# Heads and tails of the stages of a decoder-layer kernel: metered weight loads, a reordered projection loop, up-projections in a drain and a longer prologue

## The chip, the cores and the metric

One Trainium2 chip, 8 cores, one launch. Each core takes one sequence of a batch of 8, so all cores run the same program on different data and exchange nothing. The metric is the device time of the slowest core in microseconds (us), as the median of several executions. An eight-core program has a slower state in some of its executions: the cores of one die, or of both, show a lower granted TensorE clock. Those runs are left out of every comparison below; all profiles that are quoted fell in the fast state.

## The reference, cut to what matters

A decoder layer on `x` (8, 4096, 1024) in float32, with three sub-layers, each behind an RMS norm:

```python
# 1. two token mixers on one normalised input
qa, ka, va, ra, za, qb, kb, vb = split(rms_norm(x, norm_mix) @ w_in)
log_a = log_sigmoid(za @ w_gla_gate + b_gla_gate) / 16          # low-rank decay, rank 16
o_a = gla_chunked(qa * dk**-0.5, ka, va, log_a)                 # gated linear attention, 4 heads
o_a = rms_norm(o_a, gla_out_norm) * silu(ra)
qd = rope_partial(rms_norm(qb, dil_q_norm)); kd = rope_partial(rms_norm(kb, dil_k_norm))
o_b = dilated_attention(qd, kd, vb)                             # 3 groups of 8 heads of 64
h = x + (g_a * (o_a @ w_br_gla) + g_b * (o_b @ w_br_dil)) @ w_mix_out
# 2. attention from 4 heads of 256 into 256 memory tokens
k, v = split(rms_norm(mem, norm_mem) @ w_xkv)
h = h + softmax(rms_norm(norm(h) @ w_xq) @ rms_norm(k).T) @ v @ w_xo
# 3. gated MLP, 2816 wide, with a causal convolution of width 3 ahead of gelu
h = h + (gelu(conv(norm(h) @ w_a)) * (norm(h) @ w_u)) @ w_ffn_down
```

## The kernel before

A small helper `fw` records every operation with its buffers and sets the semaphores; each engine then runs its own instructions in the order in which the program wrote them. That order is therefore all the scheduling there is. Loads of activations are issued by SyncE, loads of weights by GpSimd (`q="pool"`). The 4096 tokens are 32 tiles, called chunks in the linear attention, of 128; four make a slab of 512. The stages follow one another: prologue, linear attention (32 chunks), dilated attention, merge, memory attention, FFN. The parts that the change touches:

```python
# prologue: x, all early weights (6 MB of them), and only then the small gains
for i in range(3):
    nload(i)
...
for h in range(4):
    fw.dma(wqk[h]..., q="pool")            # 4 x 512 KB, q and k of the linear attention
for j in range(4):
    fw.dma(wvr[j]..., q="pool")            # 4 x 1 MB, values and swish gate
... gains ...
for i in range(8):                         # normalise two slabs
    nstat(i); nscale(i); ntrans(i); nload(i + 3)
    if i == 3: P_za(0)                     # low-rank decay, first half
    if i == 4: P_z(0)                      # and its 8 activations
for h in range(4):
    P_e(0, h)                              # scan of the decay (DVE), two exps (ACT)
    P_qk(0, h)                             # q and k projection, multiplied by the exps

# linear attention
for c in range(NT):
    hs_ = ((), (0,), (1, 2), (3,))[c4] if nx else ()
    R_o(c)                                 # output and state of chunk c
    for h in hs_:
        P_e(s_ + 1, h)
    if nx and c4 == 0:
        P_za(s_ + 1)
    R_r(c + 1)                             # swish gate of the next chunk
    ...
    R_on(c)                                # norm of the output times gate
    for h in hs_:
        P_qk(s_ + 1, h)
    R_v(c + 1, 0); R_a(c + 1); R_v(c + 1, 1)   # values and scores of the next chunk
    ...

# first projection of the dilated stage is prepared at the last chunk
CC["gqk"] = rc_.sb("gqk", (128, 2, 8, 64), F32)      # gain of 64 values, for 8 heads and 128 partitions
for a_ in range(2):
    fw.dma(CC["gqk"][:, a_, :, :], bass.AP(..., [[0, 128], [0, 8], [1, 64]]), join=True)

# merge stage: keys and values of the memory, in slots between other work
def kv_alloc(isv):
    fw.dma(KV["w"]..., q="pool")           # 2 MB in one transfer
def kv_norm(m):
    fw.dma(mt[:, :], mem[rows(m), :])      # loaded and used in the same slot
    fw.act(junk, mt, AF.Square, accum=...)
```

After memory attention the FFN's buffers are allocated and its weights loaded; no up-projection starts before the last output projection.

Of the kernel before, what the change touches and what calls it, by code (L numbers as in the profile page):

```python
# [436 lines left out]
def build():  # L437
# [31 lines left out]
    pers = Reg(Arena(nc, LO, HI - LO), 0, 4608)  # L469
# [4 lines left out]
    gall = pers.sb("gall", (128, 140), F32)  # L474
    AB = pers.p
# [131 lines left out]
    CC = {}  # L607

    def load_wd(k, g):
        wd = ar.at("wd%d" % k, (128, 8, 3, 512), BF16, (64 + 24 * (k % 2)) * K_)  # L610
        for kc in range(0, 8, 2):
            fw.dma(wd[:, kc:kc + 2, :, :].rearrange("p c j n -> p (c j n)"),
                   V(WD["w_dil"], WD["w_dil"].t[g][:, kc * 1536:(kc + 2) * 1536]), q="pool", join=True)
        CC["wd%d" % g] = wd

    GORD = (1, 2, 0)

    def c_early():
        load_wd(0, GORD[0])
        CC["tab"] = ar.at("tabc", (128, 6, 512), F32, 120 * K_)  # L620
        fw.dma(CC["tab"][:, :, :], rope_d.full_v())

# [176 lines left out]
    for i in range(3):  # L799
        nload(i)  # L800
    for h in range(4):
        fw.memset("pool", U[h][:, :], 0.0)
    fw.dma(wz[:, :, :].rearrange("p c n -> p (c n)"), WD["w_gz"].full_v(), q="pool")
    fw.dma(wgg[:, :], SM["w_gla_gate"].full_v(), q="pool")
    fw.dma(posf[:, :], pos.full_v(), q="pool")
    for h in range(4):
        fw.dma(wqk[h][:, :, :, :].rearrange("p c w n -> p (c w n)"), V(WD["w_gqk"], WD["w_gqk"].t[h]), q="pool")
    for j in range(4):
        fw.dma(wvr[j][:, :, :].rearrange("p c n -> p (c n)"), V(WD["w_gvr"], WD["w_gvr"].t[j]), q="pool")
    gr0 = 0  # L810
    for nm_, n_ in gnames:
        src = SM[nm_].full_v()
        if nm_ == "w_ffn_conv":
            src = src.rearrange("t n -> (t n)")
        gdst = grow[gr0:gr0 + n_, :] if gr0 < 52 else grow2[gr0 - 52:gr0 - 52 + n_, :]
        fw.dma(gdst, src.rearrange("(c p) -> c p", p=128), join=True)
        gr0 += n_
    fw.dma(gon[:, :], dram_bc(SM["gla_out_norm"], 256))
    gps = PB.next()
# [4 lines left out]
    fw.ts("dve", gon[:, :], gon[:, :], 0.5, ALU.mult)  # L824
    for i in range(8):
# [4 lines left out]
        if i == 3:  # L830
            P_za(0)
        if i == 4:
            P_z(0)
    Gr = Reg(ar, g_off, g_off + 8 * K_).ring("G", 2, (128, 1024), F32)
    for h in range(4):
        P_e(0, h)
        P_qk(0, h)
# [9 lines left out]
    def c_alloc():  # L847
# [6 lines left out]
        CC["gqk"] = rc_.sb("gqk", (128, 2, 8, 64), F32)  # L854
# [8 lines left out]
        for a_ in range(2):  # L863
            nm = "dil_q_norm" if a_ == 0 else "dil_k_norm"
            a = SM[nm].t
            fw.dma(CC["gqk"][:, a_, :, :], V(SM[nm], bass.AP(a.tensor, a.offset, [[0, 128], [0, 8], [1, 64]])), join=True)
# [27 lines left out]
    def proj(it, j):  # L894
# [17 lines left out]
        fw.tt("dve", c["qg"][:, j, :, :], p_[:, :].rearrange("p (a d) -> p a d", a=8), CC["gqk"][:, j, :, :], ALU.mult,  # L912
# [73 lines left out]
    for c in range(NT):  # L986
        s_, c4 = c // 4, c % 4
        nx = s_ + 1 < NS
        i = c + 8
        hs_ = ((), (0,), (1, 2), (3,))[c4] if nx else ()  # L990
        R_o(c)
        for h in hs_:
            P_e(s_ + 1, h)
        if nx and c4 == 0:
            P_za(s_ + 1)
        if c + 1 < NT:
            R_r(c + 1)
# [11 lines left out]
        for h in hs_:  # L1009
            P_qk(s_ + 1, h)  # L1010
        if c + 1 < NT:
            R_v(c + 1, 0)
            R_a(c + 1)
            R_v(c + 1, 1)
        if i + 1 < NT:
# [10 lines left out]
        if c == 27:  # L1026
            c_early()

# [87 lines left out]
    def c_step(step):  # L1116
        i, j, k = step, step - 2, step - 3
        ok = lambda q: 0 <= q < N_
        d = step - N_
        if i == 32 + 4:  # L1120
# [59 lines left out]
    fw.dma(wmo[:, :, :].rearrange("p c n -> p (c n)"), WD["w_mo"].full_v(), q="pool")  # L1180
# [31 lines left out]
    def kv_alloc(isv):  # L1212
        KV["w"] = ar.at("wkv%d" % isv, (128, 8, 1024), BF16, 0)
        fw.dma(KV["w"][:, :, :].rearrange("p c n -> p (c n)"), V(WD["w_xkv"], WD["w_xkv"].t[isv]), q="pool")

    def kv_alloc2():
        KV["mt"] = ar.at("mt", (128, 1024), F32, 16 * K_)
        KV["mn"] = ar.at("mnT", (128, 8, 256), BF16, 20 * K_)
        KV["gk"] = ar.at("gkx", (128, 256), F32, 85 * K_)
        fw.dma(KV["gk"][:, :], dram_bc(SM["x_k_norm"], 256))  # L1220

    def kv_norm(m):
        mt = KV["mt"]
        fw.dma(mt[:, :], mem[rows(m), :])
# [3 lines left out]
        xs = ogc["xs"].next()  # L1228
        fw.ts("dve", xs[:, :], mt[:, :], ss[:, 2:3], ALU.mult)
        KV["xs%d" % m] = xs  # L1230

    def kv_trans(m):
        pt = trans8(P.next(), KV["xs%d" % m])
# [19 lines left out]
    def kv_k(m):  # L1253
# [7 lines left out]
        kn = ogc["xs"].next()  # L1261
        for h in range(4):
            fw.stt("dve", kn[:, h * 256:(h + 1) * 256], srcs[h], ss[1][:, h:h + 1], KV["gk"][:, :], ALU.mult, ALU.mult)
        KV["kn"] = kn

    def kv_kt(m):
        pt = trans8(P.next(), KV["kn"])
        fw.copy("act", KV["kmT"][:, :, m * 128:(m + 1) * 128], pt)

    def kv_wxq():  # L1270
        KV["wxq"] = ar.at("wxq", (128, 8, 1024), BF16, 0)
        for kc in range(0, 8, 4):
            fw.dma(KV["wxq"][:, kc:kc + 4, :].rearrange("p c n -> p (c n)"),
                   V(WD["w_xq"], WD["w_xq"].t[:, kc * 1024:(kc + 4) * 1024]), q="pool", join=True)

    def kv_wxo():
        KV["wxo"] = ar.at("wxo", (128, 8, 1024), BF16, 32 * K_)
        for kc in range(0, 8, 4):
            fw.dma(KV["wxo"][:, kc:kc + 4, :].rearrange("p c n -> p (c n)"),
                   V(WD["w_xo"], WD["w_xo"].t[:, kc * 1024:(kc + 4) * 1024]), q="pool", join=True)  # L1280

    kv_plan = {(4, 1): [lambda: kv_alloc(0), kv_alloc2, lambda: kv_norm(0)],
               (4, 2): [lambda: kv_trans(0), lambda: kv_norm(1)], (4, 4): [lambda: kv_trans(1), kv_alloc3],
               (5, 0): [lambda: kv_k(0)], (5, 2): [lambda: kv_kt(0), lambda: kv_k(1)],
               (5, 4): [lambda: kv_kt(1), lambda: kv_alloc(1)], (6, 2): [lambda: kv_v(0)],
               (6, 4): [lambda: kv_v(1)], (6, 6): [kv_wxq]}
    for s_ in range(NS):
        for m in range(8):
# [29 lines left out]
            for f_ in kv_plan.get((s_, m), ()):  # L1318
                f_()

# [6 lines left out]
    gq = rx.sb("gqx", (128, 256), F32)  # L1327
# [6 lines left out]
    fw.dma(gq[:, :], dram_bc(SM["x_q_norm"], 256))  # L1334
# [13 lines left out]
    XL = {}  # L1348

# [37 lines left out]
    def q_norm(i):  # L1387
        c = TC[i]
        qn = qn2r.next()
        for h in range(4):  # L1390
            fw.stt("dve", qn[:, h * 256:(h + 1) * 256], c["qs"][h], c["ss"][:, 8 + h:9 + h], gq[:, :],
# [84 lines left out]

    x2load(0)
    x2load(1)
    fw.dma(gfb[:, :], dram_bc(SM["norm_ffn"], 1024))
    for k in range(NT + 11):  # L1480
        if k < 5:
# [5 lines left out]
            if k == 3:  # L1487
                kv_wxo()
# [33 lines left out]
        if NT + 1 <= k < NT + 5:  # L1522
            up_load(13 + k - NT - 1)


    for fc in range(17, NFC):
        up_load(fc)
    x3t = F_["x3"]
    wdn = ar.at("wdn", (128, NFC, 1024), BF16, 64 * K_)
    wdsub = [wdn.sub("wdn%d" % j) for j in range(6)]  # L1530
    for j in range(6):
        c0, c1 = j * 4, min(NFC, j * 4 + 4)
        fw.dma(V(wdsub[j], wdn.t[:, c0:c1, :]).rearrange("p c n -> p (c n)"),
               V(WD["w_dn"], WD["w_dn"].t[:, c0 * 1024:c1 * 1024]), q="pool")
    yt_ = ar.at("yT", (128, NFC, 512), BF16, 108 * K_)
    ysub = [yt_.sub("yT%d" % fc) for fc in range(NFC)]
    rf = Reg(ar, 52 * K_, 64 * K_)
    c1r = rf.ring("cv1_", 2, (128, 512), F32)
    c2r = rf.ring("cv2_", 2, (128, 512), F32)
    glr = rf.ring("gl", 2, (128, 512), F32)  # L1540
    abr = Reg(ar, 44 * K_, 49 * K_).ring("abt", 2, (128, 514), F32)
    rf = Reg(ar, 130 * K_, 150 * K_)
    h2r = rf.ring("h2f", 4, (128, 1024), F32)
    hist = rf.sb("hist", (128, NFC, 2), F32)
    hsub = [hist.sub("hist%d" % fc) for fc in range(NFC)]
    for fc in range(NFC):
        fw.memset("pool", V(hsub[fc], hist.t[:, fc, :]), 0.0)
    PB = Rot(BK)
    wcb = V(gall, gall.t[:, 52:140])

# [105 lines left out]
```

## Time and profile before

| | before |
|---|---|
| median of 3 runs | 3181.96 us (3180.67 to 3182.05) |
| spans of the 8 cores, profiled execution | 3162.8 to 3178.1 us, mean 3170.7 |
| granted TensorE clock | 0.976 to 0.982 |
| PE busy on the slowest core | 2904.7 us, 91% |

Where PE stands still is in the prediction below, line by line. Two more views help. The first is PE's timeline (start and duration in us, the operation, how many; in brackets the idle time before it and what ended it), in one chunk of the linear attention of the kernel before:

```profile
221.13 3.40 PE L245 MATMUL psum<-xnT,wqk_52 128*128 128x512 bf16 x15
...
229.27 0.27 PE L245 MATMUL psum<-qe_3_76,ke_3_80 128*128 128x128 bf16 x1 [2.84 <-DVE ke_3_80 L278]
```

The last head's projection is followed by 1.9 us of value matmuls and then by the scores that need this head's keys. DVE has not yet evacuated them, and PE waits 2.84 us. The second view is the list of transfers of the whole execution (count, size of each, median us from issue to landing):

```profile
xt_61<-x SPq DMA_DIRECT2D x11, 512.0 KB, 3.8
...
gqk<-dil_q_norm SPq DMA_DIRECT2D x1, 256.0 KB, 17.1
```

Half the bytes took more than four times as long: the gain table is written as 1,024 pieces of 256 bytes. Part of its 17.1 us it shared with 3 MB of weights; the run gqk_wide_late below has the table without them.

To know where the time goes I cut every core's execution at PE's own landmarks. "Chunk 0" is the first output matmul of chunk 0; the other marks are first or last matmuls of a kind. The figures for all runs are in the ledger under "The result". For the kernel before: 90.4 us to chunk 0, 73.0 for chunks 0 to 3, 388.9 for chunks 4 to 27, 83.9 from chunk 28 to the first transposes of the dilated attention, 646.8 for its projections and scores, 580.7 for the merge stage, 81.4 from the first query projection of memory attention to its first output projection, 377.2 from there to the first down-projection of the FFN.

### The profile page before, as it was taken

What the parts mean: (1) busy time and instruction counts of PE and PEld (TensorE: products, weight loads), DVE (VectorE), ACT (ScalarE), POOL (GpSimd) and SP (SyncE); (2) the same over time, 40 slices, a digit from 0 to 9 for tenths busy, and PEclk for the clock granted to TensorE, in tenths of its full rate; (3) what the DMA queues carried; (4) which work ended last, traced back from release to release, by engine and by line L of the source; (5) the groups of instructions that cost most, each with busy time, mean ns of one, the idle gap of its engine ahead of it and who ended that gap; (6) DMA issues with size and microseconds to landing.
All of it is one profiled execution on the core that took longest, in us unless ns stands there. A gap on an engine that the chain in (4) does not pass through costs nothing.

```text
span 3178.1 us, 54582 instructions; the slowest of 8 cores (3162.8 to 3178.1 us)
## 1 busy us (share of the span) xinstructions
PE 2904.7 (91%) x17139; PEld 1465.6 (46%) x17454; DVE 1845.5 (58%) x2994; ACT 1290.9 (41%) x2521; POOL 946.6 (30%) x1434
## 2 busy tenths in 40 slices
PE   3888898599999999899899887999899999999998
PEld 1444444255666555444444443444444444444443
DVE  3666666377676778444344344666656545645744
ACT  2556555266656666522232235665212212211211
POOL 1333333266666677433233210000101100100100
PEclk9999999799999999999999999999999999999999
DMA  7111111511131322544545439446810110110110
GB/s 160 37 52 63 51 34 27 108 37 42 38 82 38 81 77 79 119 147 140 152 138 150 126 131 202 155 152 193 208 67 21 47 67 27 41 67 34 47 54 27
DMA packets 94418, 279.44 MB, mean 88 GB/s; under 512 B 12570, under 2 KB 13750, under 8 KB 89782
## 3 DMA queue, kind: packets, MB, share of 16 engines
q1 hardware_dynamic: 84742, 224.96, 20.3%
q0 software_dynamic: 9392, 50.96, 9.5%
q8 instruction: 145, 2.38, 0.3%
q14 instruction: 139, 1.14, 0.1%
HBM read 224.16 MB, written 102.63 MB: 103 GB/s over the span
## 4 chain that ended last, share of the span: by engine, by line
PE 71%; DVE 10%; issue 6%; ACT 6%; DMA 6%; SPq 0%; POOL 0%; DVEq 0%; ACTq 0%; POOLq 0%
PE psum L245 68%; PE psum L249 3%; ACT jh L271 1%; DMA gqk<-dil_k_norm 1%; DMA xt_61<-x 1%; DVE on_109 L304 1%; ACT junkX L271 1%; DMA oat<-oaT_d 1%; DMA x2i_214<-xn_d 1%; DVE cm_68 L308 1%; DMA mt<-mem 1%; DMA gon<-gla_out_norm 1%; ACT L271 0%; DVE x3s_240 L314 0%; DVE qn_2_222 L304 0%
## 5 line engine op out<-in xcount | busy, mean ns | idle before, releaser
L245 PE MATMUL psum<-wdn,yT 128*128 128x512 bf16 x1379 | 303.7, 379 | 3.0 <-DVE yT L278 1.5
L245 PEld LDWEIGHTS psum<-wdn,yT 128*128 128x128 bf16 x1408 | 137.7, 98 | 167.9 <-issue 2.0
L245 PE MATMUL psum<-wd_170,xnT 128*128 128x512 bf16 x736 | 176.7, 382 | 6.6 <-issue 6.6
L245 PE MATMUL psum<-wd_135,xnT 128*128 128x512 bf16 x737 | 176.4, 382 | 5.1 <-issue 4.9
L245 PE MATMUL psum<-wd_171,xnT 128*128 128x512 bf16 x736 | 175.2, 380 | 3.3 <-issue 2.4
L314 POOL COPY hist<-abt_279 128x2 f32<-128x2 f32 x88 | 16.2, 185 | 510.8 <-ACT abt_279 L313 510.8
L313 ACT COPY abt_279<-psum 128x512 f32<-128x512 f32 x88 | 50.1, 569 | 242.3 <-PE psum L245 235.8
L271 ACT ACTIVATE gl_278<-cv_1_274 128x512 f32<-128x512 f32 x88 | 55.4, 630 | 223.7 <-DVE cv_1_274 L304 223.7
L271 ACT ACTIVATE gl_277<-cv_0_273 128x512 f32<-128x512 f32 x88 | 55.4, 630 | 218.5 <-DVE cv_0_273 L304 218.5
L278 DVE TENSOR_TENSOR mab_193<-psum,sig_192 128x512 f32<-128x512 f32 x64 | 44.2, 691 | 148.9 <-PE psum L245 141.2
L278 DVE TENSOR_TENSOR qg_139<-psum,gqk 128x512 f32<-128x512 f32 x96 | 66.2, 689 | 110.5 <-ACT sq_137 L271 69.9
L245 PEld LDWEIGHTS psum<-wd_170,xnT 128*128 128x128 bf16 x768 | 103.0, 146 | 48.0
L278 DVE TENSOR_TENSOR qg_140<-psum,gqk 128x512 f32<-128x512 f32 x96 | 66.1, 689 | 89.6 <-ACT sq_137 L271 60.3
L245 PEld LDWEIGHTS psum<-wd_135,xnT 128*128 128x128 bf16 x768 | 81.2, 115 | 67.7 <-issue 1.9
L245 PEld LDWEIGHTS psum<-wd_171,xnT 128*128 128x128 bf16 x768 | 68.5, 98 | 74.7
L314 POOL COPY hist<-abt_280 128x2 f32<-128x2 f32 x88 | 16.3, 185 | 275.5 <-ACT abt_280 L313 275.5
L296 DVE TENSOR_SCALAR cv_0_273<-abt_279,gall 128x512 f32<-128x512 f32 x88 | 48.1, 546 | 77.6 <-ACT abt_279 L313 77.6
L271 ACT ACTIVATE sq_138<-psum 128x512 f32<-128x512 f32 x96 | 57.5, 599 | 84.4 <-PE psum L245 84.4
L296 DVE TENSOR_SCALAR cv_1_274<-abt_280,gall 128x512 f32<-128x512 f32 x88 | 48.1, 547 | 73.6 <-ACT abt_280 L313 73.6
L271 ACT ACTIVATE sig_192<-psum,gall 128x512 f32<-128x512 f32 x64 | 43.9, 687 | 109.3 <-PE psum L245 105.4
L278 POOL TENSOR_TENSOR ogl_172<-ogl_172 128x520 f32<-128x520 f32 x64 | 84.4, 1319 | 9.4 <-DMA ogl_172<-og_d 4.8
L271 ACT ACTIVATE sq_137<-psum 128x512 f32<-128x512 f32 x96 | 57.4, 598 | 61.1 <-PE psum L245 60.9
(671 smaller groups left out, 7247.1 us busy)
## 6 DMA issues: line engine op xcount, KB each, us to landing
ogl_172<-og_d SPq DMA_DIRECT2D x96, 260.0 KB, 3.6
og_d<-og_166 SPq DMA_DIRECT2D x32, 260.0 KB, 2.1
og_d<-og_167 SPq DMA_DIRECT2D x32, 260.0 KB, 2.5
og_d<-og_168 SPq DMA_DIRECT2D x32, 260.0 KB, 2.2
oaT_d<-oT_110 SPq DMA_DIRECT2D x32, 256.0 KB, 2.1
oat<-oaT_d SPq DMA_DIRECT2D x32, 256.0 KB, 4.1
xtT_199<-x SPq DMA_DIRECT2D x16, 512.0 KB, 5.3
h_d<-xtT_199 SPq DMA_DIRECT2D x16, 512.0 KB, 4.3
```

The costliest lines, as they stand in the source:

```text
L245: return self._add("pe", lambda e: e.matmul(o, l, r, start=start, stop=stop), [lhsT, rhs], [out], xr=xr)
L249: return self._add("pe", lambda e: e.transpose(o, i, d), [in_, ident], [out])
L271: return self._add("act", lambda e: e.activation(o, i, func, **kw), reads, writes, xr=xr, xw=xw)
L278: return self._add(eng, lambda e: e.tensor_tensor(o, a, b, op), [in0, in1], [out], xr=xr, xw=xw)
L296: return self._add(eng, lambda e: e.tensor_scalar(o, a, s1, s2, op0, **kw), reads, writes)
L304: return self._add(eng, lambda e: e.scalar_tensor_tensor(o, a, scalar, b, op0, op1), reads, [out])
L308: return self._add("dve", lambda e: e.tensor_tensor_scan(o, a, b, 0.0, ALU.mult, ALU.add), [d0, d1], [out])
L313: return self._add("act", lambda e: e.copy(o, i), [in_], [out])
L314: return self._add(eng, lambda e: e.tensor_copy(o, i), [in_], [out])
```

## The change

Its intent is to leave the matmuls alone and fill the gaps at the heads and tails of the stages.

1. Small gains go ahead of everything; the value and gate weights wait; q and k projections of two slabs (before: one) are done before chunk 0, in turn with the normalisation of tiles 4 to 7.
2. In the loop the projection stands right behind the output matmuls, and its scan and exponentials a chunk earlier.
3. The gain table of the dilated stage is a compact one (128 rows of 256 bytes), loaded in the prologue and read with stride 0.
4. Weight loads are cut into pieces on a list `BG`; `bg()` issues one piece at marked places ("metering").
5. Merge stage: the memory tile is loaded a slot ahead and its normalised copy has its own scratch; the key and value work is spread over other slots.
6. The first eight up-projections are written between the last tiles of memory attention; FFN buffers move to make room. Also, at the start of memory attention the gain of the queries is loaded earlier and the transposed tiles get a second buffer.

```diff
+    BG = []
+    def bg(n=1):
+        for _ in range(n):
+            if BG:
+                BG.pop(0)()
+    def bg_load(buf, name, src, pieces):
+        ...
+        for q in range(pieces):
+            BG.append(lambda q=q: fw.dma(dst[:, q * n:(q + 1) * n], ..., q="pool", join=True))
 ...
+    for i in range(4):
+        norm(i)
+    for s_ in range(2):
+        P_za(s_)
+        P_z(s_)
+        P_e(s_, 0)
+        P_e(s_, 1)
+        for h in range(4):
+            if s_ == 0:
+                norm(4 + h)
+                fw.dma(wvr[h]..., q="pool")
+            P_qk(s_, h)
+            if h < 2:
+                P_e(s_, h + 2)
 ...
-        nx = s_ + 1 < NS
+        nx = 1 <= s_ < NS - 1
         R_o(c)
-        for h in hs_:
-            P_e(s_ + 1, h)
+        if nx:
+            for h in ((), (0,), (1, 2), (3,))[c4]:
+                P_qk(s_ + 1, h)
 ...
         R_on(c)
-        for h in hs_:
-            P_qk(s_ + 1, h)
         ... R_v, R_a, R_v ...
+        if nx:
+            for h in ((0,), (1, 2), (3,), ())[c4]:
+                P_e(s_ + 1, h)
 ...
+        if c > 27:
+            bg(2)
 ...
-        fw.dma(KV["w"]..., q="pool")
+        bg_load(KV["w"], "w_xkv", WD["w_xkv"].t[isv], 4)
+    def kv_mem(m):
+        fw.dma(KV["mt"][:, :], mem[rows(m), :])
 ...
+        if k >= NT + 5:
+            for _ in range(1 if k < NT + 9 else 2):
+                cur = up(0, len(UPD))
+                ...
```

> **What bounds the kernel now.** I read the page first, from busy shares to the chain that ended last, then PE's waits, then the chain piece by piece, then busy time by window. From the page: engines, two rows of the 40 slices (79.5 us each), the chain by engine.
>
> ```profile
> PE 2904.7 (91%) x17139; PEld 1465.6 (46%) x17454; DVE 1845.5 (58%) x2994; ACT 1290.9 (41%) x2521; POOL 946.6 (30%) x1434
> ...
> PE   3888898599999999899899887999899999999998
> ...
> DMA  7111111511131322544545439446810110110110
> ...
> PE 71%; DVE 10%; issue 6%; ACT 6%; DMA 6%; SPq 0%; POOL 0%; DVEq 0%; ACTq 0%; POOLq 0%
> ```
>
> PE is the bound: 91% busy, 71% of the chain. So the change can win only where PE stands still: 3178 - 2905 = 273 us at most, and matmuls at half clock. The row of slices says where: a 3 in slice 0 (prologue), 8s through the linear attention (0.09 to 0.59 ms), a 5 at its end, single 8s and a 7 in the merge stage and the start of memory attention, an 8 at its end. From about 2330 us the FFN is solid. Where PE is low, DMA is often high. PE's waits, as totals, times, longest:
>
> ```profile
> PE psum L249 <- DVE on_109 L304: 38.9, 4, 32.9
> ...
> PE psum L249 <- DVE xsT_202 L296: 20.1, 3, 15.9
> ...
> PE psum L245 <- DVE ke_3_88 L278: 11.6, 4, 4.6
> PE psum L245 <- DVE ke_3_80 L278: 8.3, 3, 2.9
> ...
> PE psum L245 <- DVE qn_1_221 L304: 9.3, 1, 9.3
> ...
> PE psum L249 <- DVE xsX_242 L304: 8.2, 2, 4.3
> ```
>
> The list blames DVE. The chain in order of time (start, duration) shows what held DVE up: transfers.
>
> ```profile
> 43.37 15.80 DMA xt_61<-x
> ...
> 589.99 33.31 DMA gqk<-dil_k_norm
> ...
> 1573.21 17.16 DMA mt<-mem
> ...
> 1785.43 14.84 DMA oat<-oaT_d
> ...
> 1905.32 17.74 DMA x2i_214<-xn_d
> ```
>
> And windows around four of them (length, busy us of PE, PEld, DVE, ACT, POOL, clock, DMA share, GB/s):
>
> ```profile
> 600.00:620.00 20.00, 0.00 (x0) 0.00 (x0) 0.00 (x0) 0.00 (x0) 0.00 (x0) 0.53 0.29 53
> ...
> 1575.00:1600.00 25.00, 8.92 (x48) 4.59 (x48) 4.83 (x6) 2.78 (x5) 4.52 (x5) 0.66 0.82 200
> ...
> 1900.00:1925.00 25.00, 10.74 (x47) 4.22 (x46) 8.31 (x14) 8.05 (x26) 6.48 (x12) 0.67 0.87 167
> ...
> 2225.00:2250.00 25.00, 17.38 (x88) 8.34 (x90) 13.70 (x18) 6.75 (x17) 1.58 (x3) 0.86 0.70 220
> ```
>
> At 600 all engines stand still behind a 256 KB gain table while DMA is 29% busy. At 1575 and 1900 an activation tile queues behind a weight load (DMA 82 and 87%). At 2225 PE runs out of independent work.
>
> **What the Trainium skill says.** (1) "TensorE: Matmul & The Clock Gate", Part 1, What's actually happening: after an idle window of some 3.4 us the array runs at half rate until it has been busy for about as long. The trace agrees: at 68.6 us matmuls of 512 columns start 0.43 us apart, from 72 us 0.22 us apart, and granted clock falls in the windows above. A long wait costs one or two us more than its length. (2) "DMA: Bandwidth & Descriptors", Issuing engines are not separate DMA queues: all transfers share 16 engines and interleave. The trace agrees: a 512 KB tile of x lands in 3.8 us (median), but took 13.7 and 15.8 us beside the weight loads of the prologue. (3) Same page, Specifications: line rate needs 512 B or more. The gain table goes as 2 transfers of 1024 pieces of 256 B; the first landed in 17.1 us, 15 to 20 GB/s. (4) "ScalarE: Activation LUTs", What ACT_TABLE_LOAD costs: a switch of table set is about 1283 ns, with its drain about 2.66 us. The trace shows 1.28 us for the load itself.
>
> **The change part by part.**
>
> *Prologue.* Small gains go first, then x, then the q/k weights; the 4 MB of value/gate weights wait until tiles 4 to 7, and halving one gain, which kept DVE blocked till 25.4 us, moves behind. The q/k projections of slab 0 interleave with normalising tiles 4 to 7; those of slab 1 are pulled ahead. Before, chunk 0 begins at 91.3 us. After, by row durations: first three tiles by 24 us, the fourth by 27 (at 3.2 us each: scale 0.75, transposes 1.0, evacuation 1.2); low-rank gate (cold matmuls 3.6), its 8 activations 4.7, first scans and exponentials to 40; then heads. A head is a chain, not a PE stretch: evacuation 0.6, scan 1.2, two exponentials 1.2, squares 1.3, POOL 0.8, scale 0.75, transposes 1.0, 16 matmuls 3.5 to 5.3 = 10 to 12 us for two heads, about 8 for the other two: 80 us. Slab 1: gate 2 + 1, activations 5, then about 3 us a head on PE: 97. Value/gate work as before, 7.5 us: chunk 0 at about 105. So +14, although the early transfers are faster: the 64 + 12 matmuls moved in (17 us) are not free.
>
> *Chunks 0 to 3* lose those matmuls: before, 14.3 + 17.2 + 21.4 + 20.4 = 73.2 us. Chunks without projections take 9.7 and 11.0 us (chunks 28, 29); here they also carry normalisation (2 us of DVE) and rope-table work (some 3 to 4 us of DVE): 12 to 13.5 each, 53. So -20.
>
> *Chunks 4 to 27.* Projection moves straight behind the output matmuls, its scan and exponentials a chunk ahead. Before, 164.4 to 553.3 us = 388.8, or 69.3 for the first slab and 63.9 for the others; PE's work is 57.8 a slab (4 x 10.3 + 64 x 0.216 + 2.7). The waits on ke_3 (19.9 us over 7) end, since the last head is evacuated well before the scores need it; I keep 2 to 3 us a slab because DVE has 46 + 10 us of work in it: 62 + 5 x 60.4 = 364. So -25.
>
> *Into dilated attention.* The gain table is loaded once, in the prologue, as 128 rows of 256 B and read with stride 0 (same 0.69 us multiply). The transposes at 628.8 then follow at about 599: -30, plus 1 to 2 of cold clock. The first dilated weights come in 8 pieces, the last two issued during chunk 30, so the first projection may wait some 3 us; less congestion in chunk 30 (4.2 us of PE waiting) returns as much. So -31.
>
> *Merge stage.* Memory tile loaded a slot ahead, own scratch, weights in 0.5 MB pieces: the 15.9 goes, and of the waits on ogl (2.7), oat (7.6) and cold clock some 8. So -24.
>
> *Start of memory attention.* The output weights come in 8 pieces from k = 0, q gain loaded earlier, second transpose buffer. PE waited 18.3 us from 1880 to 1960; starting latency of about 5 stays, cold clock 1 comes back. So -14.
>
> *Its end.* Eight up-projections (8 x 3.45 = 27.6 us) go between the last output projections. From 2228 us: 3 x 3.45 + 4 x 0.45 + 27.6 = 40 us, so the ninth starts at 2268; before, 2252.2 + 27.6 = 2279.8. That is -12, less 1 for up to 8 table switches between the norm's exp and gelu. So -11.
>
> *FFN.* The down weights are issued later, one per up-projection from the fourteenth. 5.6 MB at the 169 GB/s of software transfers (50.96 MB in 9.5% of the span) is 33 us, with h2 loads 39, against 31 us to the last up-projection plus about 9 to the last weights: up to +2. The other 930 us are the same matmuls.
>
> Sum: +14 - 20 - 25 - 31 - 24 - 14 - 11 + 2 = -109, or **3073 us**.
>
> **Rivals.** *A. The linear attention gives nothing*: moved projections take the same PE time and DVE (65% busy there) takes over as bound, with evacuations in front of the state updates. For it: waits of DVE and ACT are small and spread. Against: the ke_3 waits have one plain cause. Then +14 - 5 - 5 in place of -31: about 3108. *B. Transfers only move*: total bytes are unchanged, and the loads meet x2, h1 and h2 tiles elsewhere (DMA stands at 1.0 from 1925 to 1975 already). Against: over most slots DMA is 20 to 50% busy. Half of 24 + 14 lost: about 3092. *C. Metered loads come too late*: the first dilated projection, or the down weights, wait 5 to 10 us each: about 3085. *D. Cold clock costs more than I counted*: with 0.92 in many windows of linear attention, filling small gaps could return 15 us more: about 3055.
>
> **Range.** Table, memory tile and drain (some 58 us, 1.8%) have named causes that go; the rest is scheduling that may come out half as large or a third larger. Range 3042 to 3112. Faster by over 2% means under 3118: only A, B and C together, or an overlooked stall, prevent it. Chances 0.94, 0.055, 0.005.
>
> **What would show it.** No gqk or mt in the chain; no window at 0 near 600; transposes of on for the last chunk about 10 us after its output matmuls. Chunk 0 at 105, chunk 4 at 158, chunk 28 at 522. Windows near 1575 and 1900 in new time above 22 of 25 us. Gelu before the last output projection, with table loads between. Wrong if chunk 0 starts past 115, if chunks 4 to 27 stay above 380, if PE waits on wd or wdn, or if the FFN's end is not a plain shift.

## The result, and the profile after

| | before | after |
|---|---|---|
| median of 4 runs | 3182.01 us (3180.67 to 3183.1) | 3090.86 us (3086.24 to 3093.63) |
| core spans, profiled execution | 3162.8 to 3178.1, mean 3170.7 | 3069.4 to 3084.7, mean 3077.4 |
| granted clock | 0.976 to 0.982 | 0.987 to 0.990 |

The ratio of after to before is 0.9712, with a 95% interval of 0.9695 to 0.9729. A ratio is the mean time of one kernel's fast runs over that of the other's of the same rounds, so it is not quite the ratio of the medians. The prediction of 3073 was 18 us too low, inside its range. The page of the kernel after, the same parts as in the prediction:

```profile
PE 2921.5 (95%) x17454; PEld 1460.7 (47%) x17454; DVE 1846.0 (60%) x2994; ACT 1296.9 (42%) x2524; POOL 952.9 (31%) x1442
...
PE   3899999899999999899999979999999999999998
...
DMA  5221111421131322644546386446721111011010
...
PE 79%; DVE 6%; ACT 6%; issue 4%; DMA 3%; POOL 0%; DVEq 0%; SPq 0%; ACTq 0%; POOLq 0%
```

The work of PE, DVE and POOL is the same within 17 us (before has some matmul records fewer: 17139 of 17454). PE's share of the chain rose from 71 to 79%. Linear attention is at 9 in the slices that it fills (the third to the seventh); the 7 that is left stands at the start of memory attention. The PE waits of the slowest core (total, times, longest):

```profile
PE psum L249 <- DVE xsA_65 L296: 27.6, 4, 10.4
...
PE psum L249 <- DVE on_110 L304: 12.4, 13, 3.3
...
PE psum L245 <- DMA wd_136<-w_dil: 5.4, 1, 5.4
...
PE psum L245 <- DMA x2i_216<-xn_d: 4.6, 1, 4.6
```

The largest entry, `on`, fell from 38.9 with one wait of 32.9 (core 0 before) to 12.4 in 13 waits of at most 3.3 (core 1 after); `ke_3` and the wait of 15.9 for the memory tile (`xsT`) are gone; a wait on dilated weights has come. The prologue's tiles (`xsA`) now lead. The chain of waits in order of time names the transfers that remain (core 0; start, duration):

```profile
4.50 13.21 DMA xt_62<-x
...
553.23 6.80 DMA wd_136<-w_dil
...
1817.52 14.49 DMA x2i_214<-xn_d
```

`gqk` and `mt` are no longer in it. Windows of the kernel after, core 0 (columns as in the prediction), in the merge stage and at the start of memory attention:

```profile
1555.00:1580.00 25.00, 24.73 (x127) 11.65 (x128) 12.15 (x17) 7.45 (x17) 10.73 (x11) 1.00 0.41 138
1805.00:1830.00 25.00, 16.55 (x89) 7.76 (x89) 13.09 (x23) 11.46 (x38) 8.59 (x16) 0.93 0.93 196
```

The merge stage is full there. The start of memory attention is not: 16.55 of 25 us, at a DMA share of 0.93.

The ledger: us between PE's landmarks, mean of the 8 cores of each profiled execution. This is my own count over the traces' PE records, not a view of the profile.

```
                        before after | gqk_   wide_  compact_ unme-  loop_  short_ dense_ no_   mem_in_ pool_ up_   best_
                                     | alone  late   late     tered  old    prol.  prol.  fill  slot    rstd  late  paced
start to chunk 0          90.4 116.5 |  95.2  115.3  115.1    117.1  117.1   99.5  100.1 117.0 117.3   117.8 117.6   93.1
chunks 0 to 3             73.0  46.6 |  73.0   46.9   46.9     46.4   46.6   61.7   46.6  46.4  46.6    46.6  46.6   47.3
chunks 4 to 27           388.9 361.7 | 388.9  362.9  362.4    361.6  389.9  360.8  362.8 361.8 361.6   362.1 361.7  362.8
chunk 28 to dilated       83.9  59.3 |  57.5   73.6   60.0     55.1   59.7   60.1   59.7  60.3  59.8    60.0  60.0   51.9
dilated                  646.8 647.1 | 647.0  647.4  647.1    653.5  646.8  647.0  647.1 647.0 647.0   647.0 647.0  647.2
merge                    580.7 550.6 | 580.0  552.6  551.5    554.2  551.1  551.0  550.4 551.0 557.8   551.5 551.5  551.0
query to first output     81.4  74.6 |  81.6   74.7   74.5     78.0   74.8   75.0   75.1  75.2  74.7    75.8  74.7   70.1
first output to down     377.2 369.7 | 375.9  370.2  370.6    369.2  369.7  367.5  370.2 372.6 368.7   367.9 370.9  368.3
down to next slab's up    38.8  39.4 |  39.1   39.3   38.5     39.1   39.3   39.3   40.1  38.3  40.2    40.3  39.7   39.9
```

How well a stage repeats is read from the kernels made from "after" that leave it alone: within 1.3 us in "start to chunk 0", "chunk 28 to dilated" and "query to first output", 2.1 in "chunks 4 to 27", 2.2 in "merge". In "first output to down" seven such kernels lie between 367.5 and 370.6 us, 3.1 apart, so a difference of 2 us cannot be read there, and 3 us only just. The times of whole runs resolve less. Where a run had few fast executions I lean on this ledger. It ends with the first slab of the FFN: what follows took 809.6 us before and 811.9 after, on every core within 0.3, which no experiment looked into.

### The profile page after: what moved, and what is told of

It is laid out like the page before. It is cut to its first block, busy times and chain, and to the rows that moved or that the text cites. A ratio compares the mean times of both kernels' runs of the same rounds, so it can differ in the third digit from the quotient of the medians.

```text
span 3084.7 us, 55023 instructions; the slowest of 8 cores (3069.4 to 3084.7 us)
## 1 busy us (share of the span) xinstructions
PE 2921.5 (95%) x17454; PEld 1460.7 (47%) x17454; DVE 1846.0 (60%) x2994; ACT 1296.9 (42%) x2524; POOL 952.9 (31%) x1442
## 4 chain that ended last, share of the span: by engine, by line
PE 79%; DVE 6%; ACT 6%; issue 4%; DMA 3%; POOL 0%; DVEq 0%; SPq 0%; ACTq 0%; POOLq 0%
PE psum L245 77%; PE psum L249 3%; ACT jh L271 1%; DMA xt_62<-x 1%; DMA wdn<-w_dn 1%; ACT junkX L271 1%; ACT L271 1%; DVE on_110 L304 1%; DVE cm_69 L308 1%; DVE x3s_242 L314 0%; DMA x2i_216<-xn_d 0%; DVE qn_0_221 L304 0%; ACT junkA L271 0%; DVE qn_2_223 L304 0%; DVE qn_1_222 L304 0%
## 5 line engine op out<-in xcount | busy, mean ns | idle before, releaser
L245 PE MATMUL psum<-wd_136,xnT 128*128 128x512 bf16 x768 | 186.0, 388 | 5.4 <-DMA wd_136<-w_dil 5.4
L245 PE MATMUL psum<-wd_170,xnT 128*128 128x512 bf16 x768 | 185.4, 384 | 0.0
L245 PE MATMUL psum<-wd_171,xnT 128*128 128x512 bf16 x768 | 182.1, 380 | 0.0
L278 DVE TENSOR_TENSOR mab_193<-psum,sig_192 128x512 f32<-128x512 f32 x64 | 44.2, 691 | 144.7 <-PE psum L245 140.5
L245 PEld LDWEIGHTS psum<-wd_171,xnT 128*128 128x128 bf16 x768 | 68.5, 98 | 74.7
L278 DVE TENSOR_TENSOR mab_194<-psum,sig_191 128x512 f32<-128x512 f32 x64 | 44.0, 688 | 66.2 <-ACT sig_191 L271 32.3
L278 POOL TENSOR_TENSOR mT_190<-mab_193,mab_194 128x512 bf16<-128x512 f32 x32 | 40.4, 1263 | 129.8 <-DVE mab_193 L278 95.4
```

Of the source, the lines that this page charges most:

```text
L245: return self._add("pe", lambda e: e.matmul(o, l, r, start=start, stop=stop), [lhsT, rhs], [out], xr=xr)
L278: return self._add(eng, lambda e: e.tensor_tensor(o, a, b, op), [in0, in1], [out], xr=xr, xw=xw)
```

## The experiments

Twelve kernels, in four calls, each call on another chip. All computed the right result. Times are medians of the fast runs. Ratios are to the kernel before, in the same rounds, with the 95% interval in brackets.

### gqk_alone: the compact gain table put alone into the kernel before

```diff
+    gqk = pers.sb("gqk", (128, 2, 64), F32)
+    fw.dma(gqk[:, 0, :], dram_bc(SM["dil_q_norm"], 64), join=True)      # in the prologue, as in the change
+    fw.dma(gqk[:, 1, :], dram_bc(SM["dil_k_norm"], 64), join=True)
-        CC["gqk"] = rc_.sb("gqk", (128, 2, 8, 64), F32)
-        ... its two wide loads ...
-        fw.tt("dve", c["qg"]..., CC["gqk"][:, j, :, :], ALU.mult, ...)
+        fw.tt("dve", c["qg"]..., gqk[:, j, :].raw(0, [[0, 8], [1, 64]]), ALU.mult, ...)
```

> The kernel before with one part of the change: the q/k gain table loaded once in the prologue in compact form (128 rows of 64 values a gain, read with stride 0). Theory: the wait before the dilated stage is this table's own, so the stretch from chunk 28 to the first transposes of the dilated stage falls from 83.9 us (mean of the cores) to about 59 to 62, and the time by 22 to 27 us, to 3155 to 3160. Rival: the burst of dilated weights (3 MB issued just behind it) held DVE up anyway, so the stall only moves to another transfer: under 10 us.

Measured: 3160.16 us, ratio 0.9941 (0.9906 to 0.9975). The stage fell from 83.9 to 57.5, by 26.4 us; the prologue took 4.8 us more: the two small loads stand ahead of the fourth tile of x, whose transposes begin at 48.43 us in place of 43.44 (core 0). The rest did not move by more than 1.3 us. One table of two gains is the whole stall that the prediction put at 30. The prediction took the 33 us wait of core 0 for all cores. Core 0 had the longest one: the same wait is 26.2 to 32.9 us over the eight cores, 29.4 in the mean, and 3.3 of it stay without the table.

### gqk_wide_late and gqk_compact_late: is it the table's shape or its place?

Both start from the kernel after. The first brings the wide table of 2 times 1,024 pieces back to its old place; the second loads the compact table there.

```diff
 # gqk_wide_late
+        CC["gqk"] = rc_.sb("gqkw", (128, 2, 8, 64), F32)
+        ... two loads with [[0, 128], [0, 8], [1, 64]], at the last chunk ...
 # gqk_compact_late: the two loads of gqk moved from the prologue to the last chunk
```

> The changed kernel with the old gain table: 2 transfers of 1024 pieces of 256 B, issued at the end of the linear attention, while the dilated weights stay metered. Theory of small pieces: each transfer takes about 17 us whatever runs beside it, so both together 30 to 34 us, and the time rises by 22 to 28 us over the changed kernel (about 3113 to 3119). Rival, congestion by the 3 MB of weights issued at once before: with these metered the table lands in under 10 us and the time rises by less than 6.

> The changed kernel with the compact table (2 transfers of 128 pieces of 256 B) issued where the old one was, at the end of the linear attention. Theory of small pieces: an eighth of the pieces takes an eighth of 17 us, about 2 us each[...], so it is there before the first projection is squared: within 4 us of the changed kernel. Rival, the place of the issue (queue behind stores, hot rows read by 8 cores): 10 us or more remain.

Measured: 3104.75 us (0.9781, 0.9719 to 0.9843) and 3087.9 us (0.9709, 0.9683 to 0.9735). The stage: 73.6 and 60.0, against 59.3. PE's waits on the output's last transposes, core 0, first of the wide and then of the compact table:

```profile
PE psum L249 <- DVE on L304: 28.7, 13, 20.0
```

```profile
PE psum L249 <- DVE on L304: 12.1, 13, 3.3
```

So the place is worth nothing (0.7 us) and the shape 13.6 to 14.3 us; the expectation for the wide table, 22 to 28 us, was too high, and its rival, under 6, is out. In the kernel before the table cost 26.4, some 12 us more. The traces of gqk_wide_late say where these went (core 0: the chain, PE's timeline, a window):

```profile
554.28 27.11 DMA gqkw<-dil_k_norm
```

```profile
559.17 7.75 PE L245 MATMUL psum<-wd,xnT 128*128 128x512 bf16 x24 [5.58 <-DMA wd<-w_dil]
```

```profile
570.00:580.00 10.00, 0.00 (x0) 0.00 (x0) 0.00 (x0) 0.00 (x0) 0.00 (x0) 0.55 0.11 29
```

The two tables land 27.1 us after the second one's issue, in place of 33.3 in the kernel before, where 3 MB of weights were issued just behind them. From this issue to DVE's first multiplication by the table pass 24.1 us, before 29.6 (means of the 8 cores, my own count): some 5 us for lighter traffic. The other 6 or so are hidden: PE now waits 5.4 to 8.5 us for the metered weights before its first projection, while the table is on its way. Without other traffic the table alone still takes 27 us, with all engines at rest and the DMA engines 11% busy: it is slow by itself. The prediction named the table only.

### unmetered: every piece issued where it was put on the list

```diff
-            BG.append(lambda q=q: fw.dma(dst[...], ..., q="pool", join=True))
+            fw.dma(dst[...], ..., q="pool", join=True)
```

> The changed kernel with every metered load of the mixer, merge and attention stages issued at once where it was only queued (same pieces, same buffers; the FFN's queue stays). Theory: metering carries the merge stage and the start of memory attention, so 10 to 20 us come back there (merge stage 552 to about 562, start of memory attention 75 to about 80), while the 5.5 us wait on the first dilated weights goes: net +6 to +15 us. Rival: the gain there came from loading the memory tile a slot ahead and from its own scratch buffer, and metering is worth nothing: within 4 us of the changed kernel, or faster by the 5.5.

Measured: 3093.09 us, ratio 0.9739 (0.9683 to 0.9794); two cores of one die ran at clock 0.98 in its profile, which shows in the dilated stage and may hold part of the other differences. Metering is worth about 3.6 us in the merge stage and 3.4 at the start of memory attention; on the six other cores it is 2.8 and 3.5. Before the dilated stage it costs 4.2: with all weights issued at once, the stage takes 55.1 in place of 59.3. The sum is close to nothing: metering by itself is not what the change gained from. The pieces stayed as they were in this run, so it says nothing of them.

### loop_order_old: the linear attention's old order, all else as after

```diff
         R_o(c)
+        for h in hs_:
+            P_e(s_ + 1, h)
-        if nx: ... P_qk(s_ + 1, h) ...
 ...
         R_on(c)
+        for h in hs_:
+            P_qk(s_ + 1, h)
-        ... P_e behind R_v, R_a, R_v ...
```

> The changed kernel with the old order inside the slabs of the linear attention (scan and exponentials just behind the output matmuls, projection matmuls behind the normalised output). Theory: the order alone is worth the 27 us between chunk 4 and chunk 28, so that stretch returns from 361.7 to about 389 us and the time rises by 25 to 28 us. Rival: it was the work of slab 1 leaving chunks 0 to 3 and less DMA traffic, or clock: under 12 us return.

Measured: 3116.21 us, ratio 0.9787 (0.9755 to 0.9819). Chunks 4 to 27 take 389.9, 28.2 more than after and within 1 us of before; every other stage is within 1 us. Its PE waits (core 0):

```profile
PE psum L245 <- DVE ke L278: 16.6, 12, 2.9
...
PE psum L249 <- DVE qe L304: 11.8, 10, 2.5
```

16.6 + 11.8 = 28.4, and neither is in the list of the kernel after: waits for the freshly evacuated keys and queries are about the whole difference. Rival A of the prediction, that DVE takes over as the bound, is out: DVE had the same work in both orders. Projections and scans were put back together; which of the two moves matters more was not tried.

### short_prologue: only one slab projected ahead

```diff
-    for s_ in range(2):
+    for s_ in range(1):
-        nx = 1 <= s_ < NS - 1
+        nx = s_ < NS - 1
```

> The changed kernel with slab 1's projections back in chunks 0 to 3 (new order inside the slab), so the prologue is short again. Theory: the longer prologue gains nothing; chunk 0 starts 20 to 24 us earlier (about 94 instead of 116.5) and chunks 0 to 3 take 66 to 70 us instead of 46.6: within 4 us of the changed kernel. Rival: filling the prologue pays, since the rope-table work of the first chunks then lies beside fewer matmuls: the time rises by 6 us or more.

Measured: 3086.66 us, ratio 0.9687 (0.9662 to 0.9713). Chunk 0 begins 17.0 us earlier and chunks 0 to 3 take 15.1 longer. The longer prologue of the change bought nothing: to chunk 4 it takes 163.1 us, the kernel before 163.4, this one 161.2.

### dense_prologue: the eight tiles first, then the heads back to back

```diff
-    for i in range(4):
+    for i in range(8):
         norm(i)
+        if i == 3:
+            P_za(0)
+        if i == 4:
+            P_z(0)
+        if i >= 4:
+            fw.dma(wvr[i - 4]..., q="pool")
 ...
         for h in range(4):
-            if s_ == 0:
-                norm(4 + h)
-                fw.dma(wvr[h]..., q="pool")
             P_qk(s_, h)
```

> The changed kernel with the eight normalising tiles of the prologue run through first and the projections of slabs 0 and 1 behind them without a tile between two heads. Theory: in the changed kernel a head waits 13 us for the next tile, whose statistics stand on ACT behind that head's exponentials, a closed loop through four engines; without it the tiles take 3.2 us each and the heads about 3.6, so chunk 0 starts at 85 to 95 instead of 116.5 and the time falls by 20 to 28 us. Rival: the prologue is bound by transfers (x tiles and 6 MB of weights), so chunk 0 stays past 105: under 12 us.

Measured: 3075.42 us, ratio 0.9652 (0.9625 to 0.9679); chunk 0 at 100.1, 16.4 us earlier, with chunks 0 to 3 unchanged at 46.6. The gain is real but smaller than expected. Why the change's own order is slow is seen in two timelines of the kernel after, core 1. PE:

```profile
56.21 6.09 PE L245 MATMUL psum<-xnT,wqk_50 128*128 128x512 bf16 x16
69.20 1.01 PE L249 MATMUL psum<-cstb,xsA_66 128*128 128x128 bf16 x8 [6.90 <-DVE xsA_66 L296]
```

and ACT:

```profile
64.84 0.63 ACT L271 ACTIVATE eTp_70<-cm_69 128x512 f32<-128x512 f32 x1 [11.49 <-DVE cm_69 L308]
...
65.90 1.04 ACT L271 ACTIVATE junkA<-xt_64 128x1024 bf16<-128x1024 f32 x1
```

The head's matmuls begin at 56.21. DVE evacuates them and only then scans the decay of the next head but one; ACT waits for this scan to 64.84; behind its two exponentials stand the squares of tile 5 (65.90); then POOL, DVE and, at 69.20, PE with the tile's transposes. So goes each of the first two heads once round four engines: 13 us, of which PE has the 16 matmuls and the transposes to do. After a wait of 7 to 10 us these matmuls take 6.09 us; the same 16 take 3.63 when the second slab's are run. With all tiles normalised first, the same 64 matmuls (62 of them in the records) run in one piece (core 2):

```profile
60.86 14.62 PE L245 MATMUL psum<-xnT,wqk 128*128 128x512 bf16 x62 [0.22 <-issue]
```

The tiles themselves still came late; the last run takes this up.

### no_fill and fill_pool_rstd: the drain of memory attention

```diff
 # no_fill: no up-projection ahead of the last output projection
-        if k >= NT + 5:
+        if k >= NT + 11:
 # fill_pool_rstd: the last four tiles' norm without Ln and Exp on ACT
+        if i >= NT - 4:
+            rstd_pool(ss, 0, 2, 1, 1024)
+        else:
             fw.act(ss[:, 1:2], ss[:, 0:1], AF.Ln, ...)
             fw.act(ss[:, 2:3], ss[:, 1:2], AF.Exp, scale=-0.5)
```

> The changed kernel without up-projections between the last output projections of memory attention (same weights, same buffers, all eight behind the drain). Theory: the filling is worth about what I measured, some 5 us of the 11 predicted, the rest going to the table switches it brings: the time rises by 4 to 7 us. Rival: it is worth the full 11 and the loss is elsewhere in memory attention: 10 us or more.

> The changed kernel with the norm statistics of the last four tiles of memory attention taken from ACT (logarithm and exponential) to POOL (power), which stands idle there, so that gelu no longer alternates with them on ACT. Theory: the seven table loads of 1.28 us in the drain, two per tile, hold the statistics up, and PE's waits there are their shadow: the stretch from the first output projection to the first down projection falls from 369.7 to 364 to 367 us. Rival: the drain waits for residual tiles from DMA, and nothing changes (within 1.5 us).

Measured: no_fill 3087.78 us, ratio 0.9696 (0.9673 to 0.972; half of its runs were slow), fill_pool_rstd 3087.68 us, 0.9685 (0.964 to 0.9731). The times tell neither apart from the kernel after. In the ledger, from the first output projection to the first down-projection: 377.2 before, 372.6 without filling, 369.7 with it, 367.9 without the table switches. So the filling is worth some 2.9 us, a quarter of what was predicted: 372.6 lies above all seven kernels that keep the stage as it was (367.5 to 370.6, mean 369.5). The 1.8 us for the switches lie inside that spread and are not shown; the expected 364 to 367 was not reached. 4.6 us come from elsewhere in the change. What the switches are, ACT's timeline of the kernel after, core 0, shows:

```profile
2137.89 1.28 ACT L271 ACT_TABLE_LOAD   x1 [3.11 <-DVE cv_0_268 L304]
...
2141.01 1.28 ACT L271 ACT_TABLE_LOAD   x1
```

Gelu for the first up-projection, then back for the norm of the next tile, and so on: 7 loads in the drain, one with fill_pool_rstd. That they cost little because PE has other tiles' work there is my reading, not tested.

### mem_in_slot: the memory tile loaded in the slot that uses it

```diff
-    kv_plan = {(4, 0): [kv_alloc2, lambda: kv_mem(0), lambda: kv_alloc(0)], (4, 1): [lambda: kv_norm(0), lambda: kv_mem(1)],
-               (4, 3): [lambda: kv_trans(0), lambda: kv_norm(1)], ...
+    kv_plan = {(4, 0): [kv_alloc2, lambda: kv_alloc(0)], (4, 1): [lambda: kv_mem(0), lambda: kv_norm(0)],
+               (4, 3): [lambda: kv_trans(0), lambda: kv_mem(1), lambda: kv_norm(1)], ...
```

> The changed kernel with the memory tile loaded in the slot that normalises it, as before the change (own scratch, metered weights kept). Metering alone was worth only some 3.5 of the 30 us gained in the merge stage. Theory: the load ahead of its use carries the rest, so without it a tile's landing of 5 to 8 us stands on ACT and PE twice and the merge stage rises from 550.6 to 558 or more (time +8 us or more). Rival: either measure suffices alone (a metered weight piece of 0.5 MB delays the tile little, and a tile loaded ahead does not mind the burst), so the stage rises by under 4 us; then the old 30 us came from both faults together.

Measured: two fast runs at 3093.29 and 3098.71, ratio 0.9712 (0.9662 to 0.9762); the merge stage takes 557.8 (555.2 to 560.8), 7.2 more than after. The early load alone is worth a quarter of the 30.1 us that the stage gained, metering alone (above) an eighth. Either of the two seems to be enough to end most of the old wait: before, the tile ran beside 2 MB of weights in one transfer and was needed at once. How the other 19 us divide between the two together, the separate scratch and the new slots was not tried.

### up_late: the up weights issued eight steps later

```diff
-        if 6 <= k < 19:
-            up_load(k - 6)
+        if 14 <= k < 27:
+            up_load(k - 14)
```

> The changed kernel with the first 13 up-projection weights loaded from step 14 to 26 of memory attention instead of 6 to 18. Theory: at its start the transfers are still saturated (share 0.93 to 1.03 in the 50 us around the first output projection), now by these weights beside the residual and x2 tiles; with them later, the stretch from the first query projection to the first output projection falls from 74.6 to 68 to 71 us. Rival: it is the output weights and the tiles' own round trip through memory, and the stretch stays within 2 us.

Inconclusive. One fast run (3090.16 us; four of five were slow, so there is no ratio), and 74.7 us for the stage, as after, where the expectation was 68 to 71. The experiment did not do what it was to do. POOL's issues in the kernel after and in this one, both core 0, first and last of the 13 loads:

```profile
1813.06 0.56 POOL L241 DMA_DIRECT2D wup_250<-w_up  x1
...
1841.62 0.53 POOL L241 DMA_DIRECT2D wup_262<-w_up  x1 [3.04 <-DMA wup_254<-w_up]
```

```profile
1823.61 2.15 POOL L241 DMA_DIRECT2D wup<-w_up  x4
...
1852.93 0.53 POOL L241 DMA_DIRECT2D wup<-w_up  x1 [2.60 <-DMA wup<-w_up]
```

Steps of this stage are some 10 us apart, so 13 loads at one a step should spread over 120 us. They went out within 29 us in both, and end waiting for one another's transfers. After the last norms of the merge stage (to 1811 us in the kernel after) POOL computes nothing here and hardly waits for another engine; a place in the program is no place in time on an engine that runs ahead. The whole burst merely begins 10 us later.

### best_paced: the parts that paid, with a real pace

Starting from the kernel after: the first tile of x ahead of the gains, the q/k weights behind the tiles, the dense order of the prologue; four pieces a chunk for the dilated weights; the norm of fill_pool_rstd; and for the late loads of memory attention a wait of POOL for DVE's latest instruction.

```diff
+    nload(0)
     ... gains ...
+    nload(1)
+    nload(2)
-    for i in range(4):
+    for i in range(8):
         norm(i)
+        if i < 4:
+            fw.dma(wqk[i]..., q="pool")
+        else:
+            fw.dma(wvr[i - 4]..., q="pool")
+        if i == 3:
+            P_za(0)
 ...
-        bg(2)
+        bg(4)                                   # while the dilated weights are on the list
 ...
-        if 6 <= k < 19:
-            up_load(k - 6)
+        if 10 <= k < 23:
+            fw.wait_for("pool", [fw.prog["dve"][-1]])
+            up_load(k - 10)
```

> A version built from what the runs so far point to; numbers are stage means. (1) Prologue: the first tile of x ahead of the gains, the q/k weights of head i behind tile i, the value/gate weights behind tiles 4 to 7, all eight tiles normalised before the first head. (2) Four background loads a chunk in place of two for the dilated weights. (3) The last four memory tiles' norm without Ln and Exp. (4) The output weights left over and the 13 up weights each issued behind a wait of POOL for DVE's latest instruction. Theory: the prologue waits because x comes late and because squares of tiles 4 to 7 stand in line behind exponentials; start to chunk 0 goes from 116.5 us (100.1 with the dense prologue alone) to 84 to 92. Rival: the 8 MB of weights bind, and it stays above 98. Chunk 28 to the dilated transposes: 59.3 to 55 to 56, since the wait of 5.4 us on the last pieces goes; rival, a DVE wait replaces it, and it stays within 1.5. Start of memory attention: theory, the up weights that POOL issued in a burst hold up x2, and 74.6 becomes 67 to 71; rival, the tile's own round trip sets it, and it stays within 2. First output to first down projection: 369.7 to 366 to 368. Together 35 to 42 us less than the changed kernel, a ratio of 0.957 to 0.961 to the kernel before; if only the prologue pays, 0.963 to 0.966.

Measured: 3051.40 us (six runs, two of them slow), ratio 0.9573 (0.9539 to 0.9608), spans 3036.0 to 3052.0 with a mean of 3043.1: 34 us under the kernel after. It is the fastest of all, and the total was expected (ratio 0.957 to 0.961), but of its four stages only one landed inside the range given for it. Stage by stage:

Prologue: chunk 0 at 93.1, just outside the 84 to 92 of the theory and below the 98 of the rival. Both are partly right. Windows of the kernel after (core 1) and of this one (core 5):

```profile
40.00:60.00 20.00, 8.64 (x27) 3.02 (x25) 5.16 (x6) 8.08 (x14) 2.09 (x5) 1.00 0.15 23
```

```profile
20.00:40.00 20.00, 6.15 (x35) 2.96 (x32) 7.86 (x8) 4.59 (x8) 4.78 (x11) 0.82 1.02 201
40.00:60.00 20.00, 11.16 (x45) 4.92 (x46) 7.59 (x8) 8.19 (x14) 2.90 (x7) 0.58 1.01 206
```

The kernel after had the transfers idle (0.15) in the middle of its prologue. Here they are full from 20 to 60 us; in the first 60 us come some 11.5 MB at about 190 GB/s (6 MB of them weights, not the 8 of the expectation). So the wait that is left seems to belong to the transfers, and fewer bytes would have to come before the first head to gain more; that was not tried.

Dilated weights: 51.9 us, 7.4 less than after and better than expected. PE's wait on them is gone from the list of waits.

Memory attention: 70.1, 4.5 less, as expected, and the pace can be seen (core 0):

```profile
1851.63 0.53 POOL L241 DMA_DIRECT2D wup<-w_up  x1 [35.78 <-DVE h1x L278]
1862.19 0.53 POOL L241 DMA_DIRECT2D wup<-w_up  x1 [10.03 <-DVE h1x L278]
```

One load every 10 us, and none before the first output projection: they also stand four steps later in the program. Output weights and up weights were paced together, so their shares are not separated. Its drain: 368.3, 1.4 less, inside the spread of that stage.

## Why the prediction was right or wrong

The sum was right within 17%: -109 predicted, -93 in the mean span, -91 in the time. Its terms, beside the ledger:

| step of the prediction | predicted | measured | |
|---|---|---|---|
| prologue | +14 | +26.1 | mis-sized |
| chunks 0 to 3 | -20 | -26.4 | mis-sized |
| chunks 4 to 27 | -25 | -27.2 | right, shown by loop_order_old |
| into dilated attention | -31 | -24.6 | mis-sized |
| merge stage | -24 | -30.1 | mis-sized |
| start of memory attention | -14 | -6.8 | wrong step |
| its end | -11 | -7.5, of which filling 2.9 | right sign, wrong size |
| FFN | +2 | +0.6, and +2.3 behind the ledger's end | right |

**Prologue.** The prediction had "first three tiles by 24 us, the fourth by 27" and heads from 40. In the kernel after (core 1) the fourth tile's transposes begin at 36.06, the decay matmuls behind it at 38.62, and the first tile of a head reaches ACT at 52.22. That is the miss of 12: the tiles came late. The first x load took 13.21 us (core 0) behind the gains and beside the weights; with x first and the weights behind it (best_paced, core 5) the first transposes begin at 12.87 in place of 23.83. The heads, about 41 us from there to the second slab, and the 25 us after it were sized well (the terms listed for the second slab add up to 100 rather than 97). What the prediction did not ask is whether this chain has to be there; dense_prologue shows that 16 us of it need not.

**Chunks 0 to 3** took 46.4 to 47.7 on all cores, 11.7 each. The prediction had left 12 to 13.5, for normalisation and table work on DVE, which are hidden. Together with the prologue the term is -0.3 where the prediction had -6.

**Into dilated attention.** The mechanism was right (gqk_alone: -26.4), the size was that of the worst core: on core 0 the table's part of the wait is 29.6. Rival C came true here: the last pieces are issued late, and the last chunk's transposes of `on` come 18.6 us after its first output matmul in place of about 10 (core 0). In the kernel after, core 0, POOL's timeline has

```profile
552.62 1.16 POOL L241 DMA_DIRECT2D wd_136<-w_dil  x2
```

behind its gate multiply, and PE waits 5.5 us for them at 560.16. The prediction allowed 3 us for this wait and thought it balanced by less congestion in chunk 30.

**Merge stage.** The wait of 15.9 went, as predicted; "some 8" for the other waits was too little by 6. The two single reversals (7.2 and 3.6) do not add up to 30, so most of it is shared or lies in the new slots, which stays open.

**Start of memory attention.** The prediction counted the PE waits there and let them go, because the output weights come in pieces from the start. It took the place in the program for the time of issue. POOL issued the last output weights and 13 up weights together, the transfer share stayed at 0.93 to 1.03, and x2 still took 14.49 us (17.74 before). This is rival B, "transfers only move", true here and in part only. best_paced shows the other half: with a pace, and a later start, the stage reaches 70.1, so -11.3 from before. The second of the skill's statements in the prediction was quoted for this very case and not applied to it: the burst that SyncE's loads of x2 met was POOL's.

**Its end.** The step "three times 3.45 plus four times 0.45 plus 27.6" took PE to be free of waits in the drain once up-projections fill it. no_fill shows that it displaces little: 2.9 us. The rest of the 7.5 was gained in steps that I had not counted there.

**Rivals and signs.** A is refuted by loop_order_old. C is true with 5.4 us for the dilated weights, and not with the 2.4 us for the down weights (core 1), where it had said 5 to 10. D's 15 us would have given 3058, not 3055. D, the clock, cannot be told apart from the waits: the granted clock rose from about 0.979 to 0.988, and no run changed it alone. Two of the prediction's own signs of being wrong came true: chunk 0 starts past 115, and PE waits on `wd` and `wdn`. A window at the start of memory attention with PE at 16.55 of 25 us, where it had asked for 22, is a third. They fell on the prologue, the way into dilated attention and memory attention; the order of the loop and the table, on which half of the sum rested, held.

The errors were of both signs and mostly cancelled: +12, -6, -2, +6, -6, +7, +4, -1 make +14. That the total came out so near is luck in part.

## What to carry to other kernels

A load's place in the program is its time of issue only on an engine that is paced by other work; on an engine that is idle, give each load a wait on the engine whose progress it is to follow. When work is interleaved "to fill", follow one turn round the engines: if a tile's squares stand behind the exponentials of the head that it is to overlap, the loop runs in series, and doing one kind first and the other in one piece is faster. Read a stall on more than one core before giving it a size, and write down a stage ledger, since a good total can hide terms that are wrong by ten microseconds either way.

## What the Trainium skill lacked or had wrong

- "DMA: Bandwidth & Descriptors", Why small descriptors are slow (HBM only): it puts the overhead of a 256-byte piece at 27%. The wide gain table, 1,024 such pieces, landed 256 KB in 17.1 us, some 15 GB/s, beside 512 KB of x in 3.8 us, some 138 GB/s. With no weights beside them, two such tables took 27.1 us, some 19 GB/s, with the DMA engines 11% busy. A factor of seven to nine is not explained there. That all pieces were read from the same 256 bytes may matter and was not tried; `gffb`, 128 rows of 4 KB all read from one row, landed 512 KB in 6.5 us in the kernel before, so a shared source alone does not make a load slow.
- No page that I found says that metering by program position fails on an idle issuing engine. Thirteen loads written some 10 us apart left within 29 us; with a wait on DVE, and four steps later, they left 10 us apart, and the stage went from 74.6 to 70.1 us.
- "ScalarE: Activation LUTs", What ACT_TABLE_LOAD costs: the load itself agrees (1.28 us). The page's total of 2.66 us with a drain is not seen where ACT's instruction before had ended: at 2141.01 (core 0 after) the load starts 0.07 us behind it and the next activation starts at 2142.31, so the switch cost 1.37 us.
